# Where streams and weights start in their rows of 256 bytes: a constant moved behind the streams' tiles

## The chip, the cores and the metric

The kernel runs on one core of a Trainium2 chip. The metric is the device time of one execution in microseconds; the time before is the median of three runs, 1802.88 us (1801.29 to 1802.92). Lower is better.

## The reference

A backbone block of two layers for 256 latent tokens and 256 context tokens, of 1024 features each, all in float32. A layer is: half a feed-forward network, a token mixer, half a feed-forward network. Each of these is preceded by a norm with a shift and a scale and followed by a gated addition; shift, scale and gate come from a product of the condition with `ada_w`.

```python
def swiglu(h, w_in, w_out):
    a, b = jnp.split(h @ w_in, 2, axis=-1)
    return (jax.nn.silu(a) * b) @ w_out
...
    for l in range(DEPTH):
        x = x + 0.5 * mx[:, 2] * swiglu(ada_norm(x, ...), ffn_w_in[l, 0], ffn_w_out[l, 0])
        hctx = hctx + 0.5 * mc[2] * swiglu(ada_norm(hctx, ...), ffn_w_in[l, 0], ffn_w_out[l, 0])
        ...  # even layer: attention and mLSTM; odd layer: gated linear attention
        x = x + 0.5 * mx[:, 8] * swiglu(ada_norm(x, ...), ffn_w_in[l, 1], ffn_w_out[l, 1])
```

The last layer's mixer and its second feed-forward network give latent tokens alone, since only these are returned.

## The kernel before

**Layout.** Everything lies feature by feature: tile `xT[k]` (128 features by 512 tokens) holds the residual stream, columns 0 to 255 the context (`CTX`), columns 256 to 511 the latent tokens (`LAT`), together `BOTH`. The normed stream that a matrix product reads is kept in two parts, `hh[k]` (rounded to float32r) and `hl[k]` (what the rounding left out). A weight tile is split into two parts in the same way, by ScalarE (L120) and VectorE (L121), into `whi` and `wlo`, or into `wspare` where tiles of a stage that are free are borrowed, or into `shi` and `slo` in the start. A product of 128 by 128 weights is three matmuls (`mm3`, L146 to L148): `whi` with `hh`, `whi` with `hl`, `wlo` with `hh`. The weight part is the stationary operand, loaded ahead by a weight load (PEld in the profile) while the matmul before it still runs; the stream is the moving operand, 512 columns wide for both streams and 256 for one. In `proj_rows` (L632 to L634) it is the other way round: the streams are stationary and the weights move.

**Stages, in order.** `ffn_phase(0, 0)` with its own start (`begin`), the even mixer, `ffn_phase(0, 1)`, `ffn_phase(1, 0)`, the odd mixer, and the last feed-forward network, which is written out at the end of the kernel. In a feed-forward stage `ffn_in` loops over 22 tiles of the hidden width; each makes two sums (`ps_ab`) of 8 by 3 matmuls, and `gated` turns them into `gh`, `gl`. The output product reads these as its moving operand and sums into `ps_y`. Where a stage begins, `gemm_first` takes the first four tiles for the context first and the latent tokens later, 256 columns at a time. Between the tiles, `ada_step` and `ada_finish` work on the modulation of later stages; their short matmuls (L190) come between the others. The order on TensorE is the order in which the program writes the matmuls.

**The last layer.** The odd mixer puts its result into the latent columns of `hh` and `hl` (`out_split`), multiplies it with the output weights (`out_mm`), and the last norm writes the same columns (`norm_steps`, `modulate`) for `ffn_in(1, 1, LAT, ...)`.

**Where tiles lie.** Each pool gives its tiles addresses in the order in which they are made, each a multiple of 32 bytes long on each partition, and pools follow one another: constants (`cp`, with the streams in it), weights (`wp`: three `raw` of 8192 bytes, two `whi` and two `wlo` of 4096), temporaries (`tp`, tiles of 1024), then the pool of the stage at hand. A weight part for 128 rows by 128 columns is 512 bytes long. In the start's pool `ssq` (32 bytes) stands ahead of `shi`; in the even mixer's pool `gb` and `gd` (4 bytes, thus 32, each) stand ahead of the tiles that `wspare` borrows.

The order of the constants before is:

```python
    eps_t = cp.tile([P, 1], F32, name="eps_t")
    one_t = cp.tile([P, 1], F32, name="one_t")            # 4 bytes, takes 32
    xT, hh, hl = ...                                       # 8 tiles of 2048 bytes each
    md = cp.tile([P, 2, 72, 2], F32, name="md")            # 1152 bytes
    amp = cp.tile([P, 2, 3, KC, 2], F32, name="amp")       # 384
    hgate = cp.tile([P, 2, 2, KC, 2], F32, name="hgate")   # 256
    lam, cs, vec, adab = ...                               # 32, 64, 320, 576
```

Of the kernel before, what the change touches and what calls it, by code (L numbers as in the profile page):

```python
# [10 lines left out]
F32 = mybir.dt.float32  # L11
F32R = mybir.dt.float32r
AF = mybir.ActivationFunctionType
ALU = mybir.AluOpType
# [3 lines left out]
P = 128  # L18
D = 1024
KC = D // P  # L20
NS = 3
T = 256
TT = 2 * T
# [4 lines left out]
NEG = -1e30  # L28
CTX = slice(0, T)
LAT = slice(T, TT)  # L30
BOTH = slice(0, TT)


@with_exitstack
def backbone_kernel(
# [28 lines left out]
    nc = tc.nc  # L64
    cp = ctx.enter_context(tc.tile_pool(name="consts", bufs=1))
# [16 lines left out]
        nc.gpsimd.memset(unit_e[:, i, i : i + 1], 1.0)  # L82
    eps_t = cp.tile([P, 1], F32, name="eps_t")
    nc.gpsimd.memset(eps_t, EPS)
    one_t = cp.tile([P, 1], F32, name="one_t")
    nc.gpsimd.memset(one_t, 1.0)

    xT = [cp.tile([P, TT], F32, name=f"xT{k}") for k in range(KC)]
    hh = [cp.tile([P, TT], F32R, name=f"hh{k}") for k in range(KC)]
    hl = [cp.tile([P, TT], F32R, name=f"hl{k}") for k in range(KC)]  # L90
    md = cp.tile([P, 2, 72, 2], F32, name="md")
    amp = cp.tile([P, 2, 3, KC, 2], F32, name="amp")
    hgate = cp.tile([P, 2, 2, KC, 2], F32, name="hgate")
    lam = cp.tile([P, 4], F32, name="lam")
    cs = cp.tile([P, KC, 2], F32, name="cs")
    vec = cp.tile([P, 79], F32, name="vec")
# [45 lines left out]
    def half(r3, m):  # L142
        return split(r3[:, :, m * P : m * P + P])

    def mm3(ps, wh, wl, ah, al, first, last):
        nc.tensor.matmul(ps, lhsT=wh, rhs=ah, start=first, stop=False)  # L146
        nc.tensor.matmul(ps, lhsT=wh, rhs=al, start=False, stop=False)  # L147
        nc.tensor.matmul(ps, lhsT=wl, rhs=ah, start=False, stop=last)  # L148

    def gemm_h(ps, w, sl):  # L150
        for k in range(KC):
            wh, wl = (t[k] if isinstance(t, list) else t[:, k] for t in w)
            mm3(ps[:, sl], wh, wl, hh[k][:, sl], hl[k][:, sl], k == 0, k == KC - 1)


    ada_units = [(l, m) for l in range(2) for m in range(9) if l or m > 1]
# [72 lines left out]

    STREAMS = ((0, CTX), (1, LAT))  # L230
    ssum = [None, None]
    pending = {}

    def gemm_first(tiles, bank):
# [11 lines left out]
        for t, w in zip(tiles, ws):  # L246
            gemm_h(t[0], w, LAT)

# [14 lines left out]
        nc.scalar.activation(dst, ms, AF.Ln, bias=eps_t[:p])  # L263
        nc.scalar.activation(dst, dst, AF.Exp, scale=-0.5)

    def modulate(l, n, i, sl, k, rstd, pool=True):
        v = 3 * n
        u = tp.tile([P, T], F32, tag="u", name="u", bufs=3)
        sh = md[:, l, v * 8 + k, i : i + 1]
        nc.vector.scalar_tensor_tensor(u, xT[k][:, sl], amp[:, l, n, k, i : i + 1], rstd, ALU.mult, ALU.mult)  # L270
        h = hh[k][:, sl]
        if pool and k % 2:
            nc.scalar.activation(u, u, AF.Identity, bias=sh)
            nc.scalar.copy(h, u)
            nc.gpsimd.tensor_tensor(hl[k][:, sl], u, h.bitcast(F32), ALU.subtract)  # L275
        else:
            nc.scalar.activation(h, u, AF.Identity, bias=sh)
            nc.vector.scalar_tensor_tensor(hl[k][:, sl], u, sh, h.bitcast(F32), ALU.add, ALU.subtract)

    def norm_steps(l, n, i, sl, bank):  # L280

        rstd = tp.tile([P, T], F32, tag="rstd", name="rstd")

        def factors():
            ps = bank("ms")
            for a, s_ in enumerate(ssum[i]):
                nc.tensor.matmul(ps[:, :T], lhsT=ones_d, rhs=s_, start=a == 0, stop=a == len(ssum[i]) - 1)
            rsqrt(rstd, ps[:, :T])

        return [factors] + [lambda k=k: modulate(l, n, i, sl, k, rstd) for k in range(KC)]  # L290

    def residual(k, ps, gate, i, sl, nxt):
        residual_at(k, ps[:, sl], gate, i, sl, nxt)
# [56 lines left out]
        nc.scalar.copy(gh, s[:, sl])  # L350
        nc.vector.tensor_tensor(gl, s[:, sl], gh.bitcast(F32), ALU.subtract)

    def ffn_in(l, f, sl, gh, gl, bank, fp, step, j0=0, spare=None):
        w_in = ffn_w_in[l, f]
        for j1 in range(j0, NJ, 2):
            js = range(j1, min(j1 + 2, NJ))
            r = [load(rows(w_in, c0 + j1 * P, len(js) * P)) for c0 in (0, DFF)]
            if spare and j1 == 0:
                ps = [[bank("ps_ab") for _ in range(2)] for _ in js]
                gemm_first(  # L360
                    [(ps[0][a], lambda a=a: half(r[a], 0)) for a in range(2)]
                    + [(ps[1][a], lambda a=a: split_spare(r[a], 1, spare)) for a in range(2)],
                    mm_bank,
                )
                for j in js:
                    gated(ps[j], gh(j), gl(j), sl, fp)
                continue
            for j in js:
                w = [half(r3, j - j1) for r3 in r]
                ps = [bank("ps_ab") for _ in range(2)]  # L370
                for a in range(2):
                    gemm_h(ps[a], w[a], sl)
                gated(ps, gh(j), gl(j), sl, fp)
            if j1 + 2 < NJ:
                step()
# [11 lines left out]
    def ffn_phase(l, f, nxt, upto, begin=None):  # L387
        with tc.tile_pool(name=f"pffn{l}{f}", bufs=1, space=PSUM) as pa:
# [4 lines left out]
            with tc.tile_pool(name=f"ffn{l}{f}", bufs=1) as fp, ExitStack() as late:  # L393
# [8 lines left out]
                for j, p in enumerate(ps):  # L402
                    gated(p, gh(j), gl(j), BOTH, fp)
                slots = [f"g{x}{j}" for j in range(NJ - 4, NJ) for x in "hl"]
# [3 lines left out]

                ffn_in(l, f, BOTH, gh, gl, bank, fp, lambda: ada(2, upto, pa, fp), len(ps), None if begin else spare)
                table(LN_EXP)  # L410
# [187 lines left out]

    def proj_fm(w, c0, n, emit, sl=BOTH):
        for mp in range(n // 2):  # L600
# [37 lines left out]
    def out_split(k, src, sl):  # L638
        nc.scalar.copy(hh[k][:, sl], src)
        nc.vector.tensor_tensor(hl[k][:, sl], src, hh[k][:, sl].bitcast(F32), ALU.subtract)  # L640
# [25 lines left out]
    def out_mm(o, w, sl, ks, start, stop):  # L666
        for n, k in enumerate(ks):
            wh, wl = (t[k] if isinstance(t, list) else t[:, k] for t in w)
            mm3(o, wh, wl, hh[k][:, sl], hl[k][:, sl], start and n == 0, stop and n == len(ks) - 1)
# [10 lines left out]
    def even_mixer(nxt):  # L680
# [91 lines left out]
        nc.vector.tensor_tensor_scan(bwd(bcum, CTX), onesb[rv, CTX], bwd(t0, CTX), 0.0, ALU.mult, ALU.add)  # L772
        nc.vector.tensor_tensor_scan(bwd(bcum, LAT), onesb[rv, LAT], bwd(t0, LAT), bcum[rv, 0:1], ALU.mult, ALU.add)
        nc.vector.scalar_tensor_tensor(ga, psg[0:H2], gb[0:H2], bcum[0:H2], ALU.add, ALU.subtract)
# [4 lines left out]
        nc.vector.tensor_tensor_scan(bwd(mst, CTX), bwd(ga, CTX), bwd(ga, CTX), 0.0, ALU.max, ALU.max)  # L779
        nc.vector.tensor_tensor_scan(bwd(mst, LAT), bwd(ga, LAT), bwd(ga, LAT), mst[rv, 0:1], ALU.max, ALU.max)  # L780
        nc.vector.tensor_tensor(mst[H2:P], mst[0:H2], bcum[0:H2], ALU.add)
# [154 lines left out]
        def emit_qk(m, ps):  # L936
            nc.scalar.copy(qk(m), ps)
            sh = mp_.tile([P, T], F32, tag="sh", name="sh", bufs=1)
            xp = qk(m)[:, LAT]
            nc.vector.stream_shuffle(sh, xp, swap)  # L940
# [113 lines left out]
        for n, (t, b) in enumerate(zip((2, 3, 0, 1), (bank_m, bank_a, mm_bank, mm_bank))):  # L1054
            p = b("ps_y")
            out_mm(p[:, LAT], ws[t], LAT, range(KC), True, True)
            residual(4 + t, p, gate, *STREAMS[1], nxt)
# [10 lines left out]
    def odd_mixer(nxt):  # L1068
# [43 lines left out]
        yo = [mp_.tile([P, T], F32, name=f"yo{e}") for e in range(8)]  # L1112
# [179 lines left out]
        for h in range(4):  # L1292
            proj_rows(w_in, 1024 + 256 * h, v, h * T)
            if h == 3:
                for k in range(4):
                    out_split(k, yo[k], LAT)
                new = taker(mp_, [f"gk{i}" for i in range(4)] + ["la0", "la1", "ex0", "ex1"])
                ws = out_weights(w_out, 0, (None, None, new, new))
            am = scores(dirs[h])
            if h < 3:  # L1300
                dirs[h + 1] = [decays(h + 1, d) for d in range(2)]
            sts = [states(h, d, *dirs[h][d][4:6]) for d in range(2)]
            head_out(h, am, [dirs[h][d][2] for d in range(2)], sts)
        ps = tiles(mm_bank)
        for ks in (range(4), (4, 5), (6, 7)):
            for k in ks:
                if k > 3:
                    out_split(k, yo[k], LAT)
            for t in range(4):
                out_mm(ps[t], ws[t], LAT, ks, ks[0] == 0 and t % 2 == 0, ks[-1] == 7 and t % 2 == 1)  # L1310
        for t in range(4):
            residual_at(t, ps[t], gate, *st, nxt)
        new = taker(mp_, ("kd0", "kd1", "spare", "ong", "wg", "wx0", "wx1", "lr"))
        ws = out_weights(w_out, 4, (new, new, None, None))
        ps = tiles(bank_c)
        for t in range(4):
            out_mm(ps[t], ws[t], LAT, range(KC), t % 2 == 0, t % 2 == 1)
            if t % 2:
                for a in (t - 1, t):
                    residual_at(4 + a, ps[a], gate, *st, nxt)  # L1320
# [5 lines left out]
    with tc.tile_pool(name="plast", bufs=1, space=PSUM) as pa, tc.tile_pool(name="last", bufs=1) as fp:  # L1326
# [2 lines left out]
            return pa.tile([P, 512], F32, tag="ff", name=name, bufs=4)  # L1329

        gh, gl = (lazy(lambda j, x=x: fp.tile([P, T], F32R, name=f"lg{x}{j}")) for x in "hl")
        for f in norm_steps(*pending.pop("norm"), mm_bank):
            f()
        fg = fp.tile([P, D], F32, name="fg")
        nc.gpsimd.dma_start(fg, final_g.partition_broadcast(P))
# [2 lines left out]
        for t in range(2):  # L1338
            for hf in range(2):
# [3 lines left out]
                        pt[:, k4 * P : k4 * P + P], xT[hf * 4 + k4][:, T + t * P : T + t * P + P], ident  # L1343
                    )
                nc.scalar.copy(xt[t][:, hf * 512 : hf * 512 + 512], pt)
        ffn_in(1, 1, LAT, gh, gl, bank, fp, lambda: None)
        table(LN_EXP)
        for hf in range(2):
            pg = mm_bank("pg")
# [7 lines left out]
        ps = [[bank("ps_l") for _ in range(2)] for _ in range(2)]  # L1357
# [15 lines left out]
        ws = {}  # L1373
        for k, t, hf in steps:
            if k not in ws:
                ws[k] = rows_split(k)
            wh, wl = ws[k]
# [74 lines left out]
```

## Time and profile before

| | before |
|---|---|
| median of three runs | 1802.88 us (1801.29 to 1802.92) |
| the profiled execution | 1805.46 us, span 1803.8 us |
| TensorE, matmuls | 1765.4 us, 98% of the span, 10087 instructions |
| TensorE, weight loads | 1503.6 us, 83% |
| VectorE | 1153.9 us, 64% |
| ScalarE | 743.3 us, 41% |
| GpSimd | 107.1 us, 6% |
| granted TensorE clock | 0.995 |
| HBM read | 259.64 MB, 145 GB/s over the span with the 1.05 MB written |

The busy time of matmuls is the time in which at least one is under way. They are pipelined: one of 512 columns is listed with some 395 ns, but the next one starts long before it ends. What a matmul costs in a dense stretch is therefore the distance from its start to the next one's start, which the timeline shows to 0.01 us: over many matmuls, the first start taken from the last and divided by the number of gaps.

### The profile page before, as it was taken

The page shows a single profiled execution, that of the slowest core. Times are in us where ns is not written, and L with a number is a line of the kernel's source. Part 1 is how long each engine was busy: PE and PEld are TensorE (multiplying, and loading weights), DVE is VectorE, ACT ScalarE, POOL GpSimd, SP SyncE. Part 2 cuts the span into 40 slices and gives each one's busy share as a digit, 9 for nine tenths or more (in the row PEclk, how much of TensorE's full clock was granted, in tenths as well). Part 3 has the DMA queues.
Part 4 walks back from the last instruction along what each step waited for, and adds up shares of the span by engine and source line. Part 5 has one row for each costly group of instructions (what it writes and reads, how often), then busy time and mean ns, then how long its engine had stood idle before and what let it go on. Part 6 is the DMA issues. An engine that isn't in the chain of part 4 may idle for free.

```text
span 1803.8 us, 24901 instructions
## 1 busy us (share of the span) xinstructions
PE 1765.4 (98%) x10087; PEld 1503.6 (83%) x10087; DVE 1153.9 (64%) x1678; ACT 743.3 (41%) x1286; POOL 107.1 (6%) x172
## 2 busy tenths in 40 slices
PE   8999999999999999999999999999999999999998
PEld 5777778899887788777788897777888998899996
DVE  5767775657669866677753486777543747855555
ACT  4422222237658853222222352222222656654443
POOL 1000000013011020000000010000000200010000
PEclk9999999999999999999999999999999999999999
DMA  9555545443121214555542344555443632235553
GB/s 295 177 187 179 177 158 192 164 132 122 47 71 47 94 48 140 182 175 182 184 142 97 129 141 163 187 187 187 140 133 101 189 117 71 89 106 191 186 190 117
DMA packets 209303, 262.30 MB, mean 145 GB/s; under 512 B 6863, under 2 KB 188662, under 8 KB 209188
## 3 DMA queue, kind: packets, MB, share of 16 engines
q1 hardware_dynamic: 208160, 259.28, 44.0%
q8 instruction: 79, 1.29, 0.3%
q0 software_dynamic: 576, 0.84, 0.2%
q10 hardware_dynamic: 452, 0.59, 0.1%
q14 instruction: 36, 0.29, 0.1%
HBM read 259.64 MB, written 1.05 MB: 145 GB/s over the span
## 4 chain that ended last, share of the span: by engine, by line
PE 85%; DVE 7%; ACT 4%; issue 2%; DMA 1%; SPq 0%; POOL 0%; ACTq 0%; POOLq 0%; DVEq 0%
PE ps_ab L146 16%; PE ps_ab L147 16%; PE ps_ab L148 16%; PE ps_y L146 7%; PE ps_y L148 7%; PE ps_y L147 7%; PE ps_fm L148 2%; PE ps_fm L146 2%; PE ps_fm L147 2%; DVE wlo L121 1%; PE po L907 1%; PE ada_ps L190 1%; PE ps_l L1382 1%; PE ps_l L1383 1%; PE ps_l L1381 1%
## 5 line engine op out<-in xcount | busy, mean ns | idle before, releaser
L120 ACT CAST whi<-raw 128x1024 fp32r<-128x1024 f32 (+1 forms) x326 | 336.0, 1031 | 849.7 <-PE ps_ab L147 497.3
L121 DVE TENSOR_TENSOR wlo<-raw,whi 128x1024 fp32r<-128x1024 f32 (+1 forms) x326 | 392.6, 1205 | 314.4 <-ACT whi L120 309.5
L146 PE MATMUL ps_ab<-hh,whi 128*128 128x512 f32 (+1 forms) x1360 | 491.3, 362 | 1.8 <-ACT whi L120 1.0
L147 PE MATMUL ps_ab<-hl,whi 128*128 128x512 f32 (+1 forms) x1360 | 490.4, 361 | 2.6 <-POOL hl L275 2.3
L148 PE MATMUL ps_ab<-hh,wlo 128*128 128x512 f32 (+1 forms) x1360 | 489.4, 360 | 0.4 <-DVE wlo L121 0.3
L178 DVE SCALAR_TENSOR_TENSOR acc<-raw_ada,cs,acc 128x1024 f32<-128x1024 f32 x224 | 276.5, 1280 | 42.8 <-DMA raw_ada<-in_ada_w_dram 42.8
L146 PEld LDWEIGHTS ps_ab<-hh,whi 128*128 128x128 f32 x1360 | 255.4, 188 | 50.1 <-ACT whi L120 6.3
L147 PEld LDWEIGHTS ps_ab<-hl,whi 128*128 128x128 f32 x1360 | 255.9, 188 | 46.0 <-POOL hl L275 2.9
L148 PEld LDWEIGHTS ps_ab<-hh,wlo 128*128 128x128 f32 x1360 | 255.7, 188 | 44.0 <-DVE wlo L121 1.0
L148 PE MATMUL ps_y<-gh,wlo 128*128 128x512 f32 (+1 forms) x660 | 229.9, 348 | 0.4
L146 PE MATMUL ps_y<-gh,whi 128*128 128x512 f32 (+1 forms) x660 | 230.0, 348 | 0.0
L147 PE MATMUL ps_y<-gl,whi 128*128 128x512 f32 (+1 forms) x660 | 228.8, 347 | 0.0
L148 PEld LDWEIGHTS ps_y<-gh,wlo 128*128 128x128 f32 x660 | 124.9, 189 | 17.7 <-DVE wlo L121 1.6
L349 DVE TENSOR_TENSOR s<-ps_ab,s 128x512 f32<-128x512 f32 (+1 forms) x88 | 54.7, 623 | 132.6 <-PE ps_ab L148 131.1
L146 PEld LDWEIGHTS ps_y<-gh,whi 128*128 128x128 f32 x660 | 124.9, 189 | 17.1 <-ACT whi L120 1.2
L147 PEld LDWEIGHTS ps_y<-gl,whi 128*128 128x128 f32 x660 | 124.9, 189 | 15.5
L257 POOL TENSOR_TENSOR ssum<-ssum,sq 128x256 f32<-128x256 f32 x25 | 26.2, 1049 | 1117.8 <-ACT sq L255 842.2
L146 PE MATMUL ps_fm<-hh,whi 128*128 128x256 f32 (+1 forms) x256 | 83.8, 327 | 0.0
L148 PE MATMUL ps_fm<-hh,wlo 128*128 128x256 f32 (+1 forms) x256 | 83.2, 325 | 0.0
L147 PE MATMUL ps_fm<-hl,whi 128*128 128x256 f32 (+1 forms) x256 | 82.9, 324 | 0.0
L632 PE MATMUL ps_v<-whi,hh 128*128 128x256 f32 x256 | 73.4, 287 | 1.3 <-ACT mv L636 1.3
L633 PE MATMUL ps_v<-wlo,hh 128*128 128x256 f32 x256 | 73.9, 289 | 0.0
(375 smaller groups left out, 2383.4 us busy)
## 6 DMA issues: line engine op xcount, KB each, us to landing
raw<-in_ffn_w_in_dram SPq DMA_DIRECT2D x84, 1024.0 KB, 5.3
raw_ada<-in_ada_w_dram SPq DMA_DIRECT2D x64, 1024.0 KB, 5.0
raw<-in_ffn_w_out_dram SPq DMA_DIRECT2D x41, 1024.0 KB, 5.0
raw<-in_even_w_in_dram SPq DMA_DIRECT2D x12, 1024.0 KB, 5.3
raw<-in_odd_w_in_dram SPq DMA_DIRECT2D x12, 1024.0 KB, 5.4
raw<-in_ffn_w_out_dram SPq DMA_DIRECT2D x15, 768.0 KB, 4.3
raw_c<-in_ada_w_dram SPq DMA_DIRECT2D x16, 512.0 KB, 7.4
raw<-in_even_w_out_dram SPq DMA_DIRECT2D x4, 1024.0 KB, 5.0
```

Source lines behind the costliest of these rows:

```text
L120: nc.scalar.copy(hi3, r3)
L121: eng.tensor_tensor(lo3, r3, hi3.bitcast(F32), ALU.subtract)
L146: nc.tensor.matmul(ps, lhsT=wh, rhs=ah, start=first, stop=False)
L147: nc.tensor.matmul(ps, lhsT=wh, rhs=al, start=False, stop=False)
L148: nc.tensor.matmul(ps, lhsT=wl, rhs=ah, start=False, stop=last)
L178: nc.vector.scalar_tensor_tensor(ada_acc[i], r3[:, k2], s, ada_acc[i], ALU.mult, ALU.add)
L190: nc.tensor.matmul(ps[32 * j : 32 * j + 32, :256], lhsT=unit_e[:, 2 * (n - first) + i], rhs=acc[i][:, j * 256 : j * 256 + 256], start=n == ...
L257: (nc.gpsimd if i and k < KC - 2 else nc.vector).tensor_tensor(ssum[i][0], ssum[i][0], sq, ALU.add)
L349: nc.vector.tensor_tensor(s[:, sl], ps[1][:, sl], s[:, sl], ALU.mult)
L632: nc.tensor.matmul(o, lhsT=ah, rhs=wh[:, k4], start=k == 0 and t % 2 == 0, stop=False)
L633: nc.tensor.matmul(o, lhsT=ah, rhs=wl[:, k4], start=False, stop=False)
L907: nc.tensor.matmul(po[:, t], lhsT=w[:, kt, (t % 2) * P : (t % 2) * P + P], rhs=v[:, kt, h * P : h * P + P], start=kt == 0, stop=kt == nk - 1,)
```

## The change

`one_t` is made after `hgate` instead of before the streams. So `xT`, `hh`, `hl`, `md`, `amp` and `hgate` lie 32 bytes lower; `lam` and all that follows, the weights among it, stay where they were. In the last layer the normed latent stream, after the last read of the normed context, is written to columns 240 to 495 of `hh` and `hl` (`LAST`) instead of 256 to 511: 16 columns, 64 bytes, lower. What is computed stays the same.

```diff
+LAST = slice(T - 16, TT - 16)
...
-    one_t = cp.tile([P, 1], F32, name="one_t")
-    nc.gpsimd.memset(one_t, 1.0)
 
     xT = [cp.tile([P, TT], F32, name=f"xT{k}") for k in range(KC)]
...
     hgate = cp.tile([P, 2, 2, KC, 2], F32, name="hgate")
+    one_t = cp.tile([P, 1], F32, name="one_t")
+    nc.gpsimd.memset(one_t, 1.0)
...
-    def gemm_h(ps, w, sl):
+    def gemm_h(ps, w, sl, at=None):
+        at = at or sl
...
-            mm3(ps[:, sl], wh, wl, hh[k][:, sl], hl[k][:, sl], k == 0, k == KC - 1)
+            mm3(ps[:, sl], wh, wl, hh[k][:, at], hl[k][:, at], k == 0, k == KC - 1)
...
-    def modulate(l, n, i, sl, k, rstd, pool=True):
+    def modulate(l, n, i, sl, k, rstd, pool=True, to=None):
...
-        h = hh[k][:, sl]
+        to = to or sl
+        h = hh[k][:, to]
...
-            nc.gpsimd.tensor_tensor(hl[k][:, sl], u, h.bitcast(F32), ALU.subtract)
+            nc.gpsimd.tensor_tensor(hl[k][:, to], u, h.bitcast(F32), ALU.subtract)
...
# the odd mixer
-                    out_split(k, yo[k], LAT)
+                    out_split(k, yo[k], LAST)
...
-                out_mm(ps[t], ws[t], LAT, ks, ks[0] == 0 and t % 2 == 0, ks[-1] == 7 and t % 2 == 1)
+                out_mm(ps[t], ws[t], LAST, ks, ks[0] == 0 and t % 2 == 0, ks[-1] == 7 and t % 2 == 1)
...
-            out_mm(ps[t], ws[t], LAT, range(KC), t % 2 == 0, t % 2 == 1)
+            out_mm(ps[t], ws[t], LAST, range(KC), t % 2 == 0, t % 2 == 1)
...
# the last feed-forward network
-        for f in norm_steps(*pending.pop("norm"), mm_bank):
+        for f in norm_steps(*pending.pop("norm"), mm_bank, LAST):
...
-        ffn_in(1, 1, LAT, gh, gl, bank, fp, lambda: None)
+        ffn_in(1, 1, LAT, gh, gl, bank, fp, lambda: None, at=LAST)
```

More of the change, by code (lines that the diff above doesn't have):

```diff
@@ L274, in modulate, with norm_steps @@
             nc.scalar.copy(h, u)
-            nc.gpsimd.tensor_tensor(hl[k][:, sl], u, h.bitcast(F32), ALU.subtract)
+            nc.gpsimd.tensor_tensor(hl[k][:, to], u, h.bitcast(F32), ALU.subtract)
         else:
             nc.scalar.activation(h, u, AF.Identity, bias=sh)
-            nc.vector.scalar_tensor_tensor(hl[k][:, sl], u, sh, h.bitcast(F32), ALU.add, ALU.subtract)
-    def norm_steps(l, n, i, sl, bank):
+            nc.vector.scalar_tensor_tensor(hl[k][:, to], u, sh, h.bitcast(F32), ALU.add, ALU.subtract)
+    def norm_steps(l, n, i, sl, bank, to=None):
         rstd = tp.tile([P, T], F32, tag="rstd", name="rstd")
@@ L288, in factors @@
             rsqrt(rstd, ps[:, :T])
-        return [factors] + [lambda k=k: modulate(l, n, i, sl, k, rstd) for k in range(KC)]
+        return [factors] + [lambda k=k: modulate(l, n, i, sl, k, rstd, to=to) for k in range(KC)]
     def residual(k, ps, gate, i, sl, nxt):
@@ L351, in gated, with ffn_in @@
         nc.vector.tensor_tensor(gl, s[:, sl], gh.bitcast(F32), ALU.subtract)
-    def ffn_in(l, f, sl, gh, gl, bank, fp, step, j0=0, spare=None):
+    def ffn_in(l, f, sl, gh, gl, bank, fp, step, j0=0, spare=None, at=None):
         w_in = ffn_w_in[l, f]
@@ L371, in ffn_in @@
                 for a in range(2):
-                    gemm_h(ps[a], w[a], sl)
+                    gemm_h(ps[a], w[a], sl, at)
                 gated(ps, gh(j), gl(j), sl, fp)
@@ L1307, in odd_mixer @@
                 if k > 3:
-                    out_split(k, yo[k], LAT)
+                    out_split(k, yo[k], LAST)
             for t in range(4):
-                out_mm(ps[t], ws[t], LAT, ks, ks[0] == 0 and t % 2 == 0, ks[-1] == 7 and t % 2 == 1)
+                out_mm(ps[t], ws[t], LAST, ks, ks[0] == 0 and t % 2 == 0, ks[-1] == 7 and t % 2 == 1)
         for t in range(4):
```

## The prediction

> **What bounds the kernel now.** I read the head of the page and the shares of the engines first, then the windows of single stages.
>
> ```profile
> span 1803.8 us, 24901 instructions
> PE 1765.4 (98%) x10087; PEld 1503.6 (83%) x10087; DVE 1153.9 (64%) x1678; ACT 743.3 (41%) x1286; POOL 107.1 (6%) x172
> ```
>
> ```profile
> 412.00:697.00 285.00, 271.59 (x1785) 241.08 (x1784) 214.88 (x473) 193.97 (x447) 43.47 (x66) 0.99 0.24 75
> 697.00:1050.00 353.00, 353.00 (x1711) 289.06 (x1710) 210.37 (x233) 102.96 (x139) 8.75 (x8) 1.00 0.46 154
> ```
>
> TensorE is the bound. The second fence (columns: window, length, then PE, PEld, DVE, ACT, POOL, granted clock, DMA share, GB/s) has the first mixer and a feed-forward stage: in the latter TensorE is busy for all of 353.00 us, VectorE for 210.37, DMA for 46%. So time is won only where a matmul takes less, and nearly all of it counts. The next view is therefore how far apart matmuls start, by timeline, in undisturbed stretches. Each pair below is the first and last start; all between are single matmuls, one after another. First 512 columns wide, streams moving (173 rows), then the same width with the gated products moving (156 rows):
>
> ```profile
> 837.68 0.39 PE L147 MATMUL ps_ab<-hl,whi 128*128 128x512 f32 x1
> ...
> 877.82 0.39 PE L148 MATMUL ps_ab<-hh,wlo 128*128 128x512 f32 x1
> ```
>
> ```profile
> 954.74 0.39 PE L147 MATMUL ps_y<-gl,whi 128*128 128x512 f32 x1
> ...
> 989.87 0.39 PE L146 MATMUL ps_y<-gh,whi 128*128 128x512 f32 x1
> ```
>
> That is 40.14/172 = 233.4 ns and 35.13/155 = 226.6 ns for the same instruction at the same granted clock, 1.00. The reader should see one difference: where the moving tile starts in its row of 256 bytes beside the weights that are loaded meanwhile, those of the next matmul. A tile takes a multiple of 32 bytes. Between streams and weights stand `md`, `amp`, `hgate`, `lam`, `cs`, `vec`, `adab`: 1152+384+256+32+64+320+576 = 2784 = 10x256+224 bytes; streams are 2048 each. So streams stand 32 bytes higher in the row than weights (+32). The gated products are tiles of 2048 bytes behind weights and temporaries that are all multiples of 256: 0, alike.
>
> Now 256 columns wide: gated products (115 rows), streams in the last layer, early (191 rows) and late (189 rows), and the stage in which weights move and streams are stationary (53 rows).
>
> ```profile
> 1020.75 0.28 PE L148 MATMUL ps_y<-gh,wlo 128*128 128x256 f32 x1
> ...
> 1034.42 0.28 PE L148 MATMUL ps_y<-gh,wlo 128*128 128x256 f32 x1
> ```
>
> ```profile
> 1648.76 0.28 PE L147 MATMUL ps_ab<-hl,whi 128*128 128x256 f32 x1
> ...
> 1670.92 0.28 PE L148 MATMUL ps_ab<-hh,wlo 128*128 128x256 f32 x1
> ```
>
> ```profile
> 1694.76 0.28 PE L148 MATMUL ps_ab<-hh,wlo 128*128 128x256 f32 x1
> ...
> 1716.90 0.28 PE L147 MATMUL ps_ab<-hl,whi 128*128 128x256 f32 x1
> ```
>
> ```profile
> 532.74 0.28 PE L634 MATMUL ps_v<-whi,hl 128*128 128x256 f32 x1
> ...
> 538.89 0.28 PE L632 MATMUL ps_v<-whi,hh 128*128 128x256 f32 x1
> ```
>
> Alike (0): 13.67/114 = 119.9 ns. At +32: 22.16/190 = 116.6 or 22.14/188 = 117.8 ns. With the parts swapped (-32): 6.15/52 = 118.3 ns. So being alike is worth 6.8 ns at 512 columns and costs 2 to 3 ns at 256.
>
> **The change part by part.** Moving `one_t` (32 bytes) behind `hgate` takes the streams 32 bytes down and leaves the weights: 2816 = 11x256 bytes lie between, so they become alike. The counts are from the groups by shape, one row of each three (L146 to L148, or L632 to L634):
>
> ```profile
> L146 PE MATMUL ps_ab<-hh,whi 128*128 128x512 f32 x944 | 374.1, 396 | 0.0
> L146 PE MATMUL ps_ab<-hh,whi 128*128 128x256 f32 x416 | 117.3, 284 | 1.8 <-ACT whi L120 1.0 <-ACT hh L274 0.4 <-ACT hh L277 0.3
> L632 PE MATMUL ps_v<-whi,hh 128*128 128x256 f32 x256 | 73.4, 287 | 1.3 <-ACT mv L636 1.3
> L146 PE MATMUL ps_fm<-hh,whi 128*128 128x256 f32 x160 | 45.3, 283 | 0.0
> L146 PE MATMUL ps_fm<-hh,whi 128*128 128x512 f32 x96 | 38.5, 401 | 0.0
> L146 PE MATMUL ps_fm<-hh,wspare 128*128 128x256 f32 x64 | 17.9, 280 | 0.0
> L146 PE MATMUL ps_ab<-hh,wspare 128*128 128x256 f32 x64 | 17.9, 279 | 0.0
> ```
>
> (1) 512 columns, +32 to alike: 3 x (944+96) = 3120 matmuls. After each interruption an alike stretch needs some matmuls to settle, so I price it by one that begins just behind the modulation's matmuls (its 166 rows from the first to the last):
>
> ```profile
> 308.61 0.40 PE L147 MATMUL ps_y<-gl,whi 128*128 128x512 f32 x1
> ...
> 346.07 0.39 PE L147 MATMUL ps_y<-gl,whi 128*128 128x512 f32 x1
> ```
>
> 37.46/165 = 227.0 ns. 3120 x (233.4 - 227.0) = -20.0 us. But are the streams' own matmuls so, in the order of `ps_ab`? The start of the kernel shows it: `ssq` (32 bytes) ahead of `shi` puts these weights alike with the streams today.
>
> ```profile
> 65.26 0.39 PE L148 MATMUL ps_ab<-hh,slo 128*128 128x512 f32 x1
> ...
> 66.62 0.40 PE L148 MATMUL ps_ab<-hh,slo 128*128 128x512 f32 x1
> ```
>
> Six gaps in 1.36 us, 226.7 ns. Here the row counts alone: the two stand 256 bytes apart in rows of 512, as the streams will to the weights.
>
> (2) 256 columns, +32 to alike. In `ps_ab` 3 x (416+64) = 1440, less the last layer's 22x2x8x3 = 1056, are 384. In `ps_fm` 480, and half of the 192 with `wspare`, 96. In `ps_y` 4x8x3 = 96, the even mixer's `out_mm` with its two tiles of `whi`, for both streams. Together 1056 x (119.9 - 116.9, between the two values above) = +3.2 us.
>
> (3) `proj_rows`, -32 to alike: 768 x (119.9 - 118.3) = +1.2 us.
>
> (4) The last layer: `LAST` starts 16 columns, 64 bytes, lower than `LAT`, so its streams stand at -64. Besides the 1056 these are `out_mm`'s 8x8x3 = 192: 1248 matmuls. The few matmuls of before at -64 are scores of the first mixer (`stk` at the row's start, the `stk2` loaded beneath 64 bytes in, behind three `den` and two `rm` of 64 each):
>
> ```profile
> 509.31 0.28 PE L853 MATMUL pS<-stk,stk 128*128 128x256 f32 x1
> ...
> 509.65 0.28 PE L854 MATMUL pS<-stk,stk 128*128 128x256 f32 x1
> ```
>
> Two more start between these; three gaps in 0.34 us are 113.3 ns; with rounding, and as a stretch may not settle at its lowest, I take 115, near this row and not near the others. The ends are 113.3 and alike's 119.9. Against 117.0 (two thirds of the stage at 116.6, one at 117.8): 1248 x (115 - 117.0) = -2.5 us, ends -4.6 and +3.6.
>
> (5) The even mixer's `wspare` lie 64 bytes above the weights (`gb` and `gd`), so there -32 becomes -64: 192 matmuls x (115 - 118.3) = -0.6 us; some 100 of 512 columns go the same way, with no row for it: between alike's gain and as much lost, +-0.7, taken as 0.
>
> (6) In the start `shi` and the streams fall out of line, to -32: 144 matmuls, which rarely run settled today. Ends 0 and 144 x 6.7 = +1.0; I take +0.4.
>
> (7) At nothing: the memset of `one_t` keeps its place in POOL's queue, no DMA and no instruction is added, and SP's queue is passed by nothing. `LAST` overlaps 16 context columns, but the last head's `proj_rows` reads each stream tile up to its last column, so `out_split` waits for the same matmul. VectorE and ScalarE touch the streams elsewhere in their rows; their work is covered (210.37 of 353.00 us), so even 3% more on them would cost nothing there. If that cover went, VectorE's splits of weights would be late next.
>
> Sum: -20.0 + 3.2 + 1.2 - 2.5 - 0.6 + 0.4 = -18.3 us. The profiled execution took 1805.46 us around its span of 1803.8, so it would be 1787.2. The median of the runs, 1802.88, is 0.14% below; there it is 1784.6.
>
> One rule speaks against all of this. The Trainium skill, in "TensorE: Matmul & The Clock Gate", section "Step-by-step: what each phase is for", says that TensorE has two independent SBUF read ports and that loading the next weights takes no read bandwidth from the running matmul. By it no start within a row would matter and the sum would be 0. The trace disagrees: 233.4 against 226.6 ns above.
>
> **The rivals.** *A: 64 bytes is the period,* so -64 is as alike as 0. Nothing in the rows excludes it but three gaps below 119.9. The last layer then pays 1248 x (119.9 - 115) = +6.1 more: 1790.7.
>
> *B: the start doesn't matter,* and 226.6 belongs to `ps_y` for another reason (its tiles, its banks). Against it: the start of the kernel reaches 226.7 in `ps_ab`, and at 256 columns the sign turns. Time: 1802.9. That rule of the Trainium skill would give the same result.
>
> *C: given back.* The loop runs faster and a split or a load comes late at each new pair of weights. Of the stages, the mixer (271.59 us TensorE of 285.00) already waits, and there (3) and part of (2) are at home, a loss that would hide as well. In the others the second engine has 40% to spare. If half of (1) went: 1794.6.
>
> *D: slower.* Streams and weights are alike in rows of 256 but half a row apart in rows of 512, where the gated products are 0 in both. If the alike stretch only holds where both agree, matmuls go on as the start's unsettled ones. Before the six gaps above stand these, all in the same places:
>
> ```profile
> 64.34 0.40 PE L148 MATMUL ps_ab<-hh,slo 128*128 128x512 f32 x1
> 64.58 0.39 PE L147 MATMUL ps_ab<-hl,shi 128*128 128x512 f32 x1
> ```
>
> A gap of 240. At that throughout, (1) becomes 3120 x 6.6 = +20.6 and the time 1825.2. The rest of the sum is +1.7, so it decides at 233.4 - 1700/3120 = 232.9 ns: a settled gap above that makes the kernel slower. Against it: the stretch does settle in the start, within some ten matmuls.
>
> **How the numbers follow.** Forecast 67%, A 14%, B 3%, C 11%, D 5%. The prediction is the forecast's 1784.6. Its own range, with the last layer at 113.3, the losses of (2) and (3) hidden in the mixers by half, or the unknowns of (4) to (6) at their other ends but A's: 1780 to 1789. To take in A and part of C it becomes 1780 to 1792. About 0.2%, 3.6 us, is what can be told from no change: faster by more than that is the forecast, A and C, 92%; within it B, 3%; slower D, 5%.
>
> **What would show it.** After the change the timeline of `ps_ab` at 512 columns has starts 226.7 ns apart in settled stretches, and the group's mean falls from 396 ns to the 390 or so of `ps_y`; `ps_v`, `ps_fm` and `ps_ab` of two streams at 256 columns go to 120 ns; `ps_ab` in the last layer reads about 115. The stage from 697 to 1050 us, with 20x2x8x3 = 960 of the 3120 in it, is 6 us shorter, with TensorE still busy throughout. Wrong would be: starts still 233 apart (B, D), 120 in the last layer (A), or new waits on `whi` and `wlo` at L146 and L148 (C).

## The result, and the profile after

The changed kernel takes 1788.27 us (median of four runs, 1785.31 to 1790.59) against 1802.9 us before (1801.29 to 1803.48): a ratio of 0.9909, 95% interval 0.9896 to 0.9922. It is faster, inside the predicted range (1780 to 1792), 3.7 us above the predicted 1784.6. In two later series of the same kernel the medians were 1786.70 and 1785.69.

The head of the page after. The profiled execution took 1790.07 us:

```profile
span 1788.4 us, 24901 instructions
PE 1748.8 (98%) x10087; PEld 1505.4 (84%) x10087; DVE 1151.9 (64%) x1678; ACT 742.8 (42%) x1286; POOL 106.7 (6%) x172
```

The same number of instructions on every engine, 16.6 us less of TensorE, and nothing of note on the others. The feed-forward stage that stood from 697 to 1050 us lies 2 us earlier at its start; its window, with the same 1711 matmuls (columns as in the prediction):

```profile
695.03:1042.02 346.99, 346.99 (x1711) 289.37 (x1710) 209.86 (x233) 102.99 (x139) 8.74 (x8) 1.00 0.47 157
```

346.99 instead of 353.00 us, TensorE busy in all of it, the granted clock 1.00 as before. What became shorter is the distance between starts. The timeline after, in the order of the prediction's pairs: `ps_ab` at 512 columns (127 rows), `ps_fm` at 256 (216 rows), `ps_v` (52 rows), the last layer (381 rows). Lines have moved: L146 to L148 are now L148 to L150, L632 is L636.

```profile
756.60 0.39 PE L150 MATMUL ps_ab<-hh,wlo 128*128 128x512 f32 x1
...
785.16 0.39 PE L150 MATMUL ps_ab<-hh,wlo 128*128 128x512 f32 x1
...
1420.56 0.28 PE L149 MATMUL ps_fm<-hl,whi 128*128 128x256 f32 x1
...
1446.36 0.39 PE L148 MATMUL ps_fm<-hh,whi 128*128 128x256 f32 x1
...
1479.63 0.28 PE L636 MATMUL ps_v<-whi,hh 128*128 128x256 f32 x1
...
1485.73 0.28 PE L636 MATMUL ps_v<-whi,hh 128*128 128x256 f32 x1
...
1634.43 0.28 PE L148 MATMUL ps_ab<-hh,whi 128*128 128x256 f32 x1
...
1677.51 0.28 PE L150 MATMUL ps_ab<-hh,wlo 128*128 128x256 f32 x1
```

28.56/126 = 226.7 ns; 25.80/215 = 120.0; 6.10/51 = 119.6 (120.0 once the first few have settled); 43.08/380 = 113.4. The first three are what the prediction took for alike; the last is the lower end of its bounds for -64, not the 115 that it took. The groups by shape say it too, less sharply, since a matmul's listed duration is its whole passage and not the distance to the next:

```profile
L148 PE MATMUL ps_ab<-hh,whi 128*128 128x512 f32 x944 | 368.9, 391 | 0.0
L148 PE MATMUL ps_ab<-hh,whi 128*128 128x256 f32 x416 | 115.6, 280 | 1.7 <-ACT whi L122 1.0 <-ACT hh L278 0.4 <-ACT hh L281 0.2
L636 PE MATMUL ps_v<-whi,hh 128*128 128x256 f32 x256 | 74.2, 290 | 1.2 <-ACT mv L640 1.2
L148 PE MATMUL ps_fm<-hh,whi 128*128 128x256 f32 x160 | 45.7, 286 | 0.0
```

396 has become 391; `ps_fm` and `ps_v` each have 3 ns more; the 256-column `ps_ab`, most of them in the last layer, 4 ns less.

**Where the time went.** Both programs issue the same matmuls in the same order, so the starts of the same matmul can be taken from each other. Negative is earlier in the changed kernel; the first row is a state, the others are what is added in the stretch:

| stretch of the program | after minus before, us |
|---|---|
| end of the start (last `shi`) | +3.5 |
| rest of the first feed-forward stage, 912 matmuls of 512 | -5.7 |
| `ffn_phase(0, 1)`, `ps_ab` at 512, 960 | -6.0 |
| `ffn_phase(1, 0)`, `ps_ab` at 512, 960 | -6.0 |
| all `ps_y` stretches of 512 and 256 columns | 0.0 |
| even mixer with the first tiles of the next stage | +0.2 |
| first tiles of `ffn_phase(1, 0)`, 256 columns | +0.6 |
| odd mixer, up to its output product | +1.2 |
| last layer, output product and `ps_ab` | -3.1 |
| end | -15.3 |

From the end of the start on that is -18.8 us. The +3.5 us of the start is chance: two other executions of the changed kernel, below, had +1.1 and -2.3 there. Of the 3.5 us, 3.0 stand already at the first matmul of `ps_ab`, here from before, from after, and from another execution of the changed kernel (`after_beside`):

```profile
20.53 1.22 PE L146 MATMUL ps_ab<-hh,shi 128*128 128x512 f32 x2
```

```profile
23.54 1.22 PE L148 MATMUL ps_ab<-hh,shi 128*128 128x512 f32 x2 [1.90 <-ACT hh L281]
```

```profile
20.50 0.73 PE L148 MATMUL ps_ab<-hh,shi 128*128 128x512 f32 x2 [0.70 <-ACT hh L281]
```

`after_beside` begins there as before does and wins its 2.3 us right behind: in the window from 14 to 26 us (first before, then `after_beside`) the granted clock was 0.72 in the one and 1.00 in the other.

```profile
14.00:26.00 12.00, 10.36 (x63) 7.45 (x62) 7.94 (x19) 6.02 (x12) 0.00 (x0) 0.72 1.18 308
```

```profile
14.00:26.00 12.00, 9.69 (x79) 6.96 (x81) 7.95 (x19) 6.71 (x13) 0.00 (x0) 1.00 1.18 309
```

From here on each execution is therefore also given from the end of its start on ("past the start"), always against the one profiled execution of before. The clock enters the even mixer's +0.2 as well: the same matmuls of the next stage's first tiles ran at half the clock in before and at the full one after (first fence before, second after), which alone is 1.3 us in favour of the change, and about as much was lost near 457 us, where after had 0.56. In `after_beside`, which had no such difference, the row is +0.6.

```profile
677.90:680.90 3.00, 3.00 (x16) 3.00 (x15) 1.97 (x6) 2.12 (x5) 0.00 (x0) 0.50 1.04 355
```

```profile
677.00:680.00 3.00, 3.00 (x28) 3.00 (x27) 2.06 (x6) 2.26 (x6) 0.00 (x0) 1.00 1.03 358
```

### The profile page after: what moved, and what is told of

The parts are those of the page before. It is cut to its first block, busy times and chain, and to the rows that moved or that the text cites. A ratio compares the mean times of both kernels' runs of the same rounds, so it can differ in the third digit from the quotient of the medians.

```text
span 1788.4 us, 24901 instructions
## 1 busy us (share of the span) xinstructions
PE 1748.8 (98%) x10087; PEld 1505.4 (84%) x10087; DVE 1151.9 (64%) x1678; ACT 742.8 (42%) x1286; POOL 106.7 (6%) x172
## 4 chain that ended last, share of the span: by engine, by line
PE 84%; DVE 8%; ACT 4%; issue 2%; DMA 2%; POOL 0%; SPq 0%; ACTq 0%; POOLq 0%; DVEq 0%
PE ps_ab L148 15%; PE ps_ab L149 15%; PE ps_ab L150 15%; PE ps_y L148 7%; PE ps_y L150 7%; PE ps_y L149 7%; PE ps_fm L150 2%; PE ps_fm L149 2%; PE ps_fm L148 2%; DVE wlo L123 2%; PE po L911 1%; ACT whi L122 1%; PE ada_ps L193 1%; PE ps_l L1386 1%; PE ps_l L1387 1%
## 5 line engine op out<-in xcount | busy, mean ns | idle before, releaser
L149 PE MATMUL ps_ab<-hl,whi 128*128 128x512 f32 (+1 forms) x1360 | 483.6, 356 | 2.6 <-POOL hl L279 2.3
L148 PE MATMUL ps_ab<-hh,whi 128*128 128x512 f32 (+1 forms) x1360 | 484.4, 357 | 1.7 <-ACT whi L122 1.0
L150 PE MATMUL ps_ab<-hh,wlo 128*128 128x512 f32 (+1 forms) x1360 | 482.5, 355 | 1.2 <-DVE wlo L123 1.1
L148 PEld LDWEIGHTS ps_ab<-hh,whi 128*128 128x128 f32 x1360 | 255.1, 188 | 44.3 <-ACT whi L122 6.6
L150 PEld LDWEIGHTS ps_ab<-hh,wlo 128*128 128x128 f32 x1360 | 255.4, 188 | 38.7 <-DVE wlo L123 1.8
L150 PE MATMUL ps_y<-gh,wlo 128*128 128x512 f32 (+1 forms) x660 | 229.9, 348 | 0.4
L148 PE MATMUL ps_y<-gh,whi 128*128 128x512 f32 (+1 forms) x660 | 230.0, 348 | 0.0
L150 PEld LDWEIGHTS ps_y<-gh,wlo 128*128 128x128 f32 x660 | 124.9, 189 | 17.6 <-DVE wlo L123 1.5
L148 PEld LDWEIGHTS ps_y<-gh,whi 128*128 128x128 f32 x660 | 124.9, 189 | 17.0 <-ACT whi L122 1.2
L353 DVE TENSOR_TENSOR s<-ps_ab,s 128x512 f32<-128x512 f32 (+1 forms) x88 | 54.7, 622 | 118.0 <-PE ps_ab L150 117.9
L148 PE MATMUL ps_fm<-hh,whi 128*128 128x256 f32 (+1 forms) x256 | 83.9, 328 | 0.0
L150 PE MATMUL ps_fm<-hh,wlo 128*128 128x256 f32 (+1 forms) x256 | 83.5, 326 | 0.0
L636 PE MATMUL ps_v<-whi,hh 128*128 128x256 f32 x256 | 74.2, 290 | 1.2 <-ACT mv L640 1.2
```

Of the source, the lines that this page charges most:

```text
L353: nc.vector.tensor_tensor(s[:, sl], ps[1][:, sl], s[:, sl], ALU.mult)
L636: nc.tensor.matmul(o, lhsT=ah, rhs=wh[:, k4], start=k == 0 and t % 2 == 0, stop=False)
```

## The experiments

The theory was the prediction's: the place of the moving tile in its row of 256 bytes, relative to the weights that are loaded meanwhile, sets the distance between starts; alike is best at 512 columns, 64 bytes lower best at 256. The rivals: absolute places decide; a shorter period; the gain has other causes.

**The same kernel again.**

> The changed kernel once more, unchanged, in more rounds. Its profiled run reached the end of the start (the last matmul of ps_ab with shi) 3.5 us later than before's, and gained 18.8 us from there on. If that lateness is chance (when the first loads land and when the clock is granted), runs spread over some 4 us, 1785 to 1791, their median lies 14 to 18 us under before, and another profile has the start at another time. If it comes with the addresses, every run and profile has it, the end of the start lies at 70.2 us again and the median at 1788 or above.

Measured: 1786.70 us (1784.10 to 1787.57), ratio 0.9906 [0.9891, 0.9922]. The median of before beside this run and the next three was 1805.35 us, so the gain was 18.7 us, a little more than the 14 to 18 expected. The end of the start came 1.1 us late, and past it the gain was 19.4 us. So the gain belongs to the change and the start's lateness doesn't.

**Only the constant moved.**

```diff
-LAST = slice(T - 16, TT - 16)
+LAST = LAT
```

> one_t moved, the last layer's streams left in the latent columns: alike with the weights. If the place of the moving tile beside the weights decides, matmuls of 512 columns stay at 226.7 ns, and the last layer's 1248 of 256 columns start 119.9 ns apart instead of 113.3: 8.2 us more than the changed kernel, 1795 to 1797. If the last layer became faster for another reason (its tiles moved with all streams), it stays at 113.3 and the time at 1788.

Measured: 1792.51 us (1790.85 to 1794.35), ratio 0.9941 [0.9926, 0.9956]; past the start -11.1 us, 7.8 less than after. The median lies under the 1795 to 1797 that were expected: it is 5.8 us above that of the changed kernel beside it, and the start of the profiled execution came 2.2 us earlier than in before, not later. In the last layer of this kernel (383 rows) the streams are alike:

```profile
1632.17 0.28 PE L148 MATMUL ps_ab<-hh,whi 128*128 128x256 f32 x1
...
1678.00 0.28 PE L149 MATMUL ps_ab<-hl,whi 128*128 128x256 f32 x1
```

45.83/382 = 120.0 ns against 113.4: over 1248 matmuls 8.2 us, and 7.8 were found. This is rival A's difference: 64 bytes lower is not alike.

**Only the last layer's place.** The constant stays ahead of the streams; 24 columns are 96 bytes, from +32 to -64.

```diff
 one_t ahead of the streams, as before
+LAST = slice(T - 24, TT - 24)
```

> one_t where it was before, the last layer's streams 24 columns lower (96 bytes), so that they stand 64 bytes under the weights' place as in the changed kernel. If the relation decides: 113.3 ns in the last layer, 233.4 ns for 512 columns, and 1248 x (117.0 - 113.3) = 4.6 us less than before, 1798. If the last layer needs the streams alike elsewhere: no gain, 1802.

Measured: 1800.48 us (1797.86 to 1803.87, ten runs), ratio 0.9981 [0.9969, 0.9992]; past the start -4.4 us. That is 4.9 us under the 1805.35 of before beside it, where 4.6 were expected. Its last layer (384 rows):

```profile
1645.91 0.28 PE L148 MATMUL ps_ab<-hh,whi 128*128 128x256 f32 x1
...
1689.33 0.37 PE L150 MATMUL ps_ab<-hh,wlo 128*128 128x256 f32 x1
```

43.42/383 = 113.4 ns, while 512 columns stayed at 233.3. Term (4) alone is worth 1248 x (117.0 - 113.4) = 4.5 us where no wait interferes, not 2.5. This kernel moves nothing but the columns in which one layer's stream is kept, and still gains: the plainest evidence against rival B.

**Streams and weights shifted together by 64 bytes.**

```diff
+    gap = cp.tile([P, 16], F32, name="gap")
+    nc.gpsimd.memset(gap, 0.0)
     ident = cp.tile([P, P], F32, name="ident")
```

> The changed kernel with a tile of 64 bytes ahead of all constants: every tile stands 64 bytes further, all relations between streams and weights stay. If the relation alone decides, all distances stay (226.7, 119.9, 113.3 ns, and 117.8 for the even mixer's borrowed tiles) and the time is that of the changed kernel within 3 us. If the place itself counts, distances change: the last layer's streams, now at 192 in their row with weights at 0, would run at the 117.8 ns that the borrowed tiles show at just these places, 5.5 us more.

Measured: 1785.80 us (1784.83 to 1787.01), ratio 0.9906 [0.9890, 0.9923]; past the start -19.2 us. Every settled distance is that of after; the last layer (383 rows), whose streams now begin at byte 192 of the row and its weights at byte 0, where they began at 128 and 192 in the changed kernel:

```profile
1630.53 0.28 PE L150 MATMUL ps_ab<-hh,whi 128*128 128x256 f32 x1
...
1673.83 0.28 PE L151 MATMUL ps_ab<-hl,whi 128*128 128x256 f32 x1
```

43.30/382 = 113.4 ns. The relation between the two operands decides, not where either stands. In all stretches compared here `whi` and `wlo` start at the same place of a row, so whether it is the weights being loaded that count, as the theory has it, or those in use, no run tells.

**Four other relations, one run each.** Each moves the streams against the weights; the last layer is set apart by its own slice, so that a kernel shows two relations. The kernel before ran at 1804.09 us beside them.

```diff
 base_m64
+    gap = cp.tile([P, 16], F32, name="gap")        # behind hgate, beside one_t: streams at -64, last layer at -128
 base_m128
-    amp = ...  (384 bytes, behind md)
+    amp = ...  (ahead of xT: streams at +128, last layer at +64)
 base_p64
+    cs = ...   (64 bytes, ahead of xT: streams at +64), LAST = slice(T - 56, TT - 56): last layer at +96
 base_p96
+    cs, lam    (96 bytes, ahead of xT: streams at +96), LAST = slice(T - 48, TT - 48): last layer at -96
```

> A tile of 64 bytes between streams and weights: streams 64 bytes under the weights' place everywhere, 128 under it in the last layer. If the relation in 256 bytes decides and -64 is good at any width: about 220 ns at 512 columns (512 and 16 cycles instead of 32), 113.3 ns in the mixers at 256. If -64 is good at 256 columns alone, 233.3 ns as in the few matmuls with the mixer's gates. If 64 bytes is the period at 512: 226.7. The last layer at -128 is unknown: 119.9 if 128 is a period, else between 113 and 120.

> amp moved ahead of the streams: they stand 128 bytes off the weights' place, 64 above it in the last layer. If 128 bytes is a period, 226.7 ns at 512 columns and 119.9 at 256 in the mixers, as alike; if 256 is, 233 ns or another value at 512. The last layer at +64: 119.9 if only the distance modulo 64 counts, about 117.5 by some twelve scattered matmuls of the first mixer.

> cs moved ahead of the streams: 64 bytes above the weights' place, 96 above it in the last layer. If above and below are alike, the mixers at 256 columns run at 113.3 and 512 columns as in the kernel with -64; if not, 117 to 118 and some 233. The last layer at +96: if only the distance modulo 64 counts, as -32, 118.3.

> cs and lam moved ahead of the streams: 96 bytes above the weights' place, 96 under it in the last layer. If only the distance modulo 64 counts: 233.3 ns at 512 columns, 116.6 to 118.3 at 256 as at +-32. If 256 bytes is the period, values of their own; for all of them the whole time then lies between 1780 (a relation better than alike at 512) and 1815.

Measured, one execution each: 1804.45, 1805.31, 1793.12 and 1810.14 us; past the start -0.9, +1.0, -11.1 and +4.7 us. `ps_ab` at 512 columns in base_p64 (191 rows):

```profile
873.91 0.39 PE L149 MATMUL ps_ab<-hl,whi 128*128 128x512 f32 x1
...
917.41 0.39 PE L150 MATMUL ps_ab<-hh,wlo 128*128 128x512 f32 x1
```

43.50/190 = 228.9 ns, better than +32 and worse than alike. In the other three the same rows are 233.3 apart. And base_m64, where `ps_ab` in the first tiles of a stage (166 rows) and `ps_fm` (215 rows) have the same relation, -64:

```profile
1056.41 0.28 PE L151 MATMUL ps_ab<-hl,whi 128*128 128x256 f32 x1
...
1075.84 0.28 PE L151 MATMUL ps_ab<-hl,wspare 128*128 128x256 f32 x1
...
1433.37 0.28 PE L151 MATMUL ps_fm<-hl,whi 128*128 128x256 f32 x1
...
1457.64 0.28 PE L152 MATMUL ps_fm<-hh,wlo 128*128 128x256 f32 x1
```

19.43/165 = 117.8 and 24.27/214 = 113.4 ns: one relation, two distances, each held for the whole stretch. The same happens at +64, in `ps_fm` of base_p64 (143 rows), where the stretch just before these, 214 gaps at the same relation, had 117.8:

```profile
1444.91 0.28 PE L149 MATMUL ps_fm<-hl,whi 128*128 128x256 f32 x1
...
1461.00 0.28 PE L150 MATMUL ps_fm<-hh,wlo 128*128 128x256 f32 x1
```

16.09/142 = 113.3 ns. All settled distances of these kernels, before and after:

| offset, bytes | 512 columns, ns | 256 columns, ns |
|---|---|---|
| 0 | 226.7 | 120.0 |
| +32 | 233.3 | 116.7 or 117.8 |
| -32 | 233.3 | 118.3 |
| +64 | 228.9 | 117.8, seldom 113.3 |
| -64 | 233.3 | 113.3, less often 117.8 |
| +96 | 233.3 | 120.0 |
| -96 | not seen | 117.3, 118.7 or 120.0 |
| 128 | 233.3 | 118.7 or 120.0 |

No period of 64 or 128 bytes is in it: +64, -64 and 128 differ from 0, and the sign counts, for 64 at 512 columns and for 32 at 256. Whatever in these expectations went by such a period fell. Of the eight steps of 32 bytes in a row of 256 the change has the best of the seven seen at 512 columns, and in the last layer the one that reaches the lowest distance at 256 most often.

**A third arrangement from the map.** +64 for the streams costs 2.2 ns at 512 columns, but makes 256 columns faster and puts `ps_v` at -64; the last layer stays at -64.

```diff
-    cs = ...   (behind lam)
+    cs = ...   (ahead of xT)
+LAST = slice(T - 32, TT - 32)
```

> cs (64 bytes) stands ahead of the streams, beside one_t behind hgate: the streams of both widths stand 64 bytes above the weights. LAST is slice(T - 32, TT - 32): the last layer's streams stand 64 bytes below the weights, as in the changed kernel. Theory (the relation alone decides, and the map of the one-look kernels holds): settled distances 228.9 ns at 512 columns, 117.8 in ps_fm and the two-stream ps_ab of 256, 113.3 in ps_v and in the last layer. Against the changed kernel: 512 columns 3144 x 2.2 = +6.9 us, 256 columns 1056 x (117.8 - 120.0) = -2.3, ps_v 768 x (113.3 - 120.0) = -5.1 at most, since the odd mixer waits for other things too: between -0.5 and +3 us, 1786 to 1790 us, a ratio of 0.991 to 0.993 to the kernel before. Rival (a stretch of 256 columns seldom reaches its lowest pattern at -64): ps_v at 117.8 or above, and the time 1790 to 1792.

The changed kernel ran beside it:

> The changed kernel once more, on the chip of the other run of this call, so that the two can be compared. Both theories: the ratio to the kernel before of the runs so far, 0.9906 to 0.9909, and distances of 226.7 ns at 512 columns, 120.0 at 256, 113.3 in the last layer. If the gain from the end of the start on is the change's, it is again 18.8 to 19.4 us; if the end of the start comes earlier or later than before by a few us, that differs from run to run and is no part of it.

Measured: 1788.63 us (1787.63 to 1792.78), ratio 0.9912 [0.9899, 0.9924], against 1785.69 us (1784.23 to 1787.39), ratio 0.9894 [0.9878, 0.9909], for the changed kernel: 2.9 us slower, at the upper end of what was expected. Past the start the two differ by less, -17.8 us against -18.3: of the 3.0 us between their profiled executions 2.6 had arisen in the start, so most of the 2.9 may be the start's chance. That the changed kernel's ratio lies under the expected 0.9906 to 0.9909 may have the same reason, since its start came 2.3 us early. Its `ps_v` (60 rows) does run as the map says:

```profile
528.85 0.28 PE L636 MATMUL ps_v<-whi,hh 128*128 128x256 f32 x1
...
535.54 0.28 PE L638 MATMUL ps_v<-whi,hl 128*128 128x256 f32 x1
```

6.69/59 = 113.4 ns instead of 120.0. But across the odd mixer's `ps_v` part the kernel gains only 0.2 us over the one before, where these matmuls were at 118.3. At least part of the rest meets other waits earlier: TensorE's waits for VectorE there come to 4.0 us instead of 2.9. The loss at 512 columns is paid in full: `ps_ab` of `ffn_phase(1, 0)` gains 4.1 us over before instead of 6.0. No arrangement was found that clearly beats the change, and past the start this one comes within 0.5 us of it.

## Why the prediction was right, and where not

Past the start its terms (1) to (5) add up to -18.7 us; the changed kernel's three executions have -18.8, -19.4 and -18.3. That these meet so closely is partly luck, for errors of both signs cancel: in the first execution 17.7 us of term (1)'s 20.0 can be seen, terms (2) and (3) with what else lies in the mixers and first tiles came to +2.0 where they alone were to be +4.4, and term (4) to -3.1 instead of -2.5.

**Term (1), right.** 226.7 ns was measured, 227.0 taken. In the 2832 `ps_ab` matmuls it gave 5.7 + 6.0 + 6.0 = 17.7 us; 2832 x 6.4 would be 18.1. The other 288, in `ps_fm`, lie in the mixers, and there nothing can be told apart.

**Terms (2) and (3), right in price, partly hidden.** 120.0 ns for 256 columns alike, in `ps_ab`, `ps_fm` and `ps_v`. The first tiles of `ffn_phase(1, 0)` paid 0.6 us, 167 of their matmuls 3.3 ns each. Of `proj_rows` the odd mixer shows only 0.1 us, where 384 matmuls at 1.7 ns would be 0.7: most did not reach the time, as the prediction's range allowed for and its sum did not.

**Term (4), mis-sized.** The step that failed is "as a stretch may not settle at its lowest, I take 115, near this row and not near the others". It settled at 113.4 over 380 gaps. The three gaps of before had pointed there, but 0.34 us between two starts shown to 0.01 us is anything from 110 to 117 ns each. By that it is 4.5 us and not 2.5. The changed kernel's execution got 3.1 of them; the waits and the timeline of that stage (1634 to 1690 us) show most of the reason:

```profile
ACT whi L122 <- DMA raw<-in_ffn_w_in_dram: 3.1, 1, 3.1
PEld ps_ab L150 <- DVE wlo L123: 1.3, 2, 1.0
PE ps_ab L150 <- DVE wlo L123: 0.8, 1, 0.8
```

```profile
1677.83 0.39 PE L148 MATMUL ps_ab<-hh,whi 128*128 128x256 f32 x1
1678.05 0.28 PE L149 MATMUL ps_ab<-hl,whi 128*128 128x256 f32 x1
1679.09 0.39 PE L150 MATMUL ps_ab<-hh,wlo 128*128 128x256 f32 x1 [0.76 <-DVE wlo L123]
```

One load of weights came late, ScalarE's split waited 3.1 us for it, VectorE's after it, and TensorE stood for about 1 us behind them. That is rival C's mechanism, at a tenth of its price. It comes and goes: over the last layer the changed kernel's three executions gained 3.1, 3.7 and 3.0 us, and last_only 4.4. The 3.0, in `after_beside`, have another cause. TensorE did not wait for weights there, but the last 357 matmuls of `ps_ab`, at 113.4 ns in every other execution with -64, ran so:

```profile
1672.59 0.28 PE L148 MATMUL ps_ab<-hh,whi 128*128 128x256 f32 x1
...
1714.52 0.28 PE L150 MATMUL ps_ab<-hh,wlo 128*128 128x256 f32 x1
```

41.93/356 = 117.8 ns: the same kernel, the same instructions, and the stretch held the other distance to its end. That cost 1.6 us. So the reason that the prediction gave for 115 was not empty: such a stretch need not settle at its lowest. In the last layer it mostly does.

**Term (5), wrong.** The even mixer's `wspare` at -64 were taken at 115. After, in `ps_fm` (49 rows):

```profile
416.49 0.28 PE L150 MATMUL ps_fm<-hh,wlo 128*128 128x256 f32 x1
...
422.15 0.28 PE L150 MATMUL ps_fm<-hh,wspare 128*128 128x256 f32 x1
```

5.66/48 = 117.9 ns: the other of the two distances at -64, as in the even mixer of every execution of the changed kernel. By that the 192 matmuls gain 0.1 us, not 0.6. The 512-column ones that go the same way stayed at 233.3, so they lost nothing and gained nothing.

**Term (6), right in kind.** The start's `shi`, now at -32, run 233.3 ns apart (7.00 us over 30 gaps at the end of the start). What that costs can't be read, since the start's end moves by 6 us between executions of one kernel. The first series' median lies 3.7 us above the prediction and the two later ones 1.1 and 2.1 above it, less than this spread.

**The rivals.** A falls by one_t_only (120.0 against 113.4 in the same matmuls). B falls by last_only and shift64: 233.3 or 226.7 ns for one instruction follow from where the two operands stand to each other. The Trainium skill says in "TensorE: Matmul & The Clock Gate", section "Step-by-step: what each phase is for", that loading the next weights takes no read bandwidth from the running matmul. What the prediction drew from it, that no start would matter, does not hold here; whether read bandwidth is what is lost, no run shows. C is there with about 1 us. D falls: half a row apart in rows of 512 the stretches settle at 226.7 as the gated products do. Its price was also too high. The gap of 240 lies between two starts shown to 0.01 us, the later of them at 64.58; the four gaps of before from the start at 63.65 to that one are 232.5 ns each, not more than the settled 233.4:

```profile
63.65 0.39 PE L147 MATMUL ps_ab<-hl,shi 128*128 128x512 f32 x1
```

## What to carry to other kernels

Where TensorE is busy throughout, compare the distance between starts of the same instruction in different stages, not its listed duration; a difference at the same clock is something to find. Here it is the address of the moving tile in its row of 256 bytes relative to the weights loaded beside it, and the best relation depends on the width, so measure each width and count the matmuls of each before a tile is moved. A small constant ahead of large tiles, or a shift by a few columns, sets it for a whole kernel at no cost; a gain in a stage that waits for other engines may not reach the time, as `ps_v` shows. All of this was seen with weights of 128 by 128 in float32r, new for each matmul; nothing else was tried.

## What was not expected of the hardware

Four of the settled distances lie on a grid of 6.67 ns: 113.33, 120.0, 226.67 and 233.33 are 17, 18, 34 and 35 steps of it. The others, such as 117.8, 118.7 and 228.9, don't; 117.8 is the mean of a pattern that repeats: 118, 118, 117, 118, 118, 118, 117, 119, 117. At -64 and at +64 and 256 columns there are two distances with one relation (113.3 and 117.8), each stable for a hundred matmuls and more. In `after_beside` the long stretch of the last layer at 117.8 began 0.16 us behind the matmul before it, where the same place in the four other executions that were compared (after, after_again, last_only, shift64) had 0.21 or 0.22 and then 113.3. But that gap alone does not choose the pattern: in the first tiles of that layer a short stretch of 15 gaps began 0.22 us behind in `after_again` and `last_only` and ran at 117.8, where four other executions (after, `after_beside`, shift64, after_third) began with the same gap and ran at 113.3. What chooses it, and why the relation counts at all, stays open.
